# Ten small vector loads move from the sync engine's DMA queue to the scalar engine's

## The chip, the cores and the metric

The program runs on one core of one Trainium2 chip. The number that counts is the device time in microseconds of one execution. The core has five instruction streams: TensorE (PE), VectorE (DVE), ScalarE (ACT), GpSimd (POOL) and the sync engine (SP, which only issues transfers). Each stream is executed in order. An instruction that waits holds up whatever stands behind it in its own stream.

## The reference

Two layers of a streaming encoder over 1024 tokens of width 1024, with 256 memory tokens. The part that matters here is the start of layer A, and the vectors that go with it:

```
mem_n = layer_norm(mem, mem_ln_g, mem_ln_b)
u, qm, gate = split(x @ a_w_in)                      # u: 2 x 1536 channels
a, gl = split(u);  h = a * sigmoid(gl)
h = causal depthwise conv, 31 taps (a_conv_w) + a_conv_b
y_mix = silu(layer_norm(h, a_ln_g, a_ln_b))
...
y_mem = cross attention of qm into mem_n
x = layer_norm(ALPHA * x + concat(y_mix, y_mem) * silu(gate) @ a_w_out)
```

Layer B is sparse attention: an indexer scores the keys, the 256 best per query are kept, 12 heads attend to them. It ends with the same kind of output projection and LayerNorm. All of it is in float32.

## The kernel before

Every float32 matrix product is done as three products of float32r parts (hi by hi, hi by lo, lo by hi). A weight piece of 128 by 512 words is loaded (L122), rounded into `wh` by ACT (L131), and its remainder `wl` is formed by POOL (L132). There are three buffers for the raw pieces, so the fourth load of a piece has to wait until POOL has finished with the first.

The kernel starts by loading x in eight blocks of 128 tokens (`x_load`, L244, tiles `xn`). Each block is transposed on PE into a PSUM tile `px` (L249, two such tiles), then ACT writes the hi part `xhi` (L168) and DVE the lo part `xlo` (L169). The first projection needs the first four blocks, which are the first 512 tokens, and the first two weight pieces, which are the gate columns of `u_pair(0)`. Pieces three and four are the `a` columns of the same pair. `project_steps` issues the 24 products of half a projection (L149, L151, L153).

The change touches `rows_load`. It gathers the per-channel vectors as rows of two small tiles: 31 taps, conv bias, LN gain and LN bias for channels 0 to 1023 (`rows0`) and 1024 to 1535 (`rows1`), and the memory LayerNorm's gain and bias (`rows0`). They are ten loads. `rows_in` transposes them on PE (L267) and DVE copies the result into `chan` (L268). The users of `chan` are the memory tokens' LayerNorm (L290), the convolution (L423, L433) and the gate of the convolution's output (L613).

The order of the instructions on each engine isn't the order of the source. A planner runs through the program with modelled durations and gives an engine that is free the ready instruction with the highest priority, and priority follows the source. What has nothing to wait for can thus go out early on an idle engine. Before the change every transfer of the program was issued by SP. The completion of transfers is signalled over a small set of counters that are handed out in turn, and a counter that is still in use is waited for at the next issue that gets it.

Of the kernel before, what the change touches and what calls it, by code (L numbers as in the profile page):

```python
# [18 lines left out]
PSUM = bass.MemoryType.PSUM  # L19

P = 128
T = 1024
# [5 lines left out]
TAPS = 31  # L28
# [36 lines left out]
def trunk(ctx, tc, x, mem, mem_g, mem_b, a_w_in, conv_w, conv_b, ln_g, ln_b,  # L65
          a_w_mkv, a_w_out, a_pg, a_pb, b_w_in, b_w_mkv, b_w_out, b_pg, b_pb, out, dbg=None):
    nc = tc.nc
# [13 lines left out]
    # ---------------------------------------------------------------- constants  # L81
# [7 lines left out]
    # per-channel vectors, channel on the partition: taps, conv bias, LN gain, LN bias, mem gain, mem bias  # L89
# [12 lines left out]
    # PSUM banks: projections ("pj") and the rest ("pt"), from the pools of the phase  # L102
# [14 lines left out]
    # ---------------------------------------------------------------- helpers  # L117
    def split_w(src3, shape, place=None, pool_only=False):
        """Loads a [128, 512]-word piece of a weight and splits it into two float32r parts."""
        n = uid()  # L120
        raw = wp.tile(shape, F32, tag="wraw", bufs=3, name=f"wr{n}")
        nc.sync.dma_start(raw, src3)  # L122
        if place is None:
            hi = wp.tile(shape, F32R, tag="whi", bufs=6, name=f"wh{n}")
            lo = wp.tile(shape, F32R, tag="wlo", bufs=6, name=f"wl{n}")
        else:
            hi, lo = place(n)
        if pool_only:
            nc.gpsimd.tensor_copy(hi, raw)
        else:  # L130
            nc.scalar.activation(hi, raw, AF.Copy)  # L131
        nc.gpsimd.tensor_tensor(lo, raw, hi.bitcast(F32), op=OP.subtract)  # L132
        return hi, lo

    def load_cols(w, c0, n=P, pool_only=False):
        """Columns c0:c0+n of a [1024, C] weight as two pieces of four 128-row blocks."""
        res = []
        for g in range(2):
            res.append(split_w(w[g * 512:(g + 1) * 512, c0:c0 + n].rearrange("(k p) c -> p k c", p=P), [P, 4, n],
                               pool_only=pool_only))  # L140
        return res

    def project_steps(pieces, mhi, mlo, c0, n, o):
        """o[cols, n] = W^T X over the moving operand's columns c0:c0+n, one product at a time."""
        for k in range(KD):
            hi, lo = pieces[k // 4]
            wh, wl = hi[:, k % 4, :], lo[:, k % 4, :]
            xh, xl = mhi[:, k, c0:c0 + n], mlo[:, k, c0:c0 + n]
            nc.tensor.matmul(o, wh, xh, start=(k == 0), stop=False)  # L149
            yield  # L150
            nc.tensor.matmul(o, wh, xl, start=False, stop=False)  # L151
            yield
            nc.tensor.matmul(o, wl, xh, start=False, stop=(k == KD - 1))  # L153
            yield

    def run(steps):
        """All that is left of some steps, and what they return."""
        while True:
            try:
                next(steps)  # L160
            except StopIteration as end:
                return end.value
# [12 lines left out]
    def ln_moments(src):  # L175
        """Mean and 1/sqrt(var + eps) of [128, 1024] along the free axis."""
        n = uid()
        st = small.tile([P, 2, 6], F32, tag="bnst", name=f"bnst{n}")
        for i in range(2):
            nc.vector.bn_stats(st[:, i, :], src[:, i * 512:(i + 1) * 512])  # L180
        mv = small.tile([P, 2], F32, tag="bnmv", name=f"bnmv{n}")
        nc.vector.bn_aggr(mv, st)
        rs = small.tile([P, 1], F32, tag="bnrs", name=f"bnrs{n}")
        nc.scalar.activation(rs, mv[:, 1:2], AF.Sqrt, bias=eps)
        nc.vector.reciprocal(rs, rs)
        return mv[:, 0:1], rs

    def ln_stats(src):
        """Scale and bias that normalize."""
        mean, rs = ln_moments(src)  # L190
        nb = small.tile([P, 1], F32, tag="bnnb", name=f"bnnb{uid()}")
        nc.vector.tensor_scalar(nb, mean, rs, -1.0, op0=OP.mult, op1=OP.mult)
        return rs, nb
# [7 lines left out]
    def layer_norm_late(dst, src, g, b, o):  # L201
        """The same in fewer steps, written out by halves."""
# [7 lines left out]
    def transpose_in(src, hi, lo, t, f=None):  # L210
        """[128 tok, 1024] -> columns t*128.. of the transposed hi and lo operands."""
# [11 lines left out]
    # ================================================================ layer A  # L223
    SC = {}
    with ExitStack() as actx:
# [14 lines left out]
        # ---- x and the vectors  # L240
# [13 lines left out]
        def rows_load():  # L254
            nc.gpsimd.memset(rows[1][32:, :], 0.0)
            for i, sl in enumerate((slice(0, T), slice(T, CONV_CH))):
                nc.sync.dma_start(rows[i][:TAPS, :], conv_w[:, sl])
                for j, v in enumerate((conv_b, ln_g, ln_b)):
                    nc.sync.dma_start(rows[i][TAPS + j:TAPS + j + 1, :], v[sl].unsqueeze(0))
            for j, v in enumerate((mem_g, mem_b)):  # L260
                nc.sync.dma_start(rows[0][TAPS + 3 + j:TAPS + 4 + j, :], v.unsqueeze(0))
# [8 lines left out]
        # ---- memory tokens: LN, transposed  # L270
# [23 lines left out]
        def mem_k(w, h, kv=None, raw=None):  # L294
            """K^T of one head of the memory attention, into kv = [K hi | V hi | K lo | V lo] or raw = [K | V]."""
# [8 lines left out]
        def mem_v(w, h, kv=None, raw=None):  # L304
            """V of one head, likewise."""
# [13 lines left out]
        def silu_gate(pl, w, c0, dst):  # L319
            """silu of 128 gate columns, transposed, into dst [128, 1024]."""  # L320
# [6 lines left out]
        def mem_q(pl, tags, pc):  # L327
            """Queries of one head, transposed, in two parts; the products one at a time."""
# [9 lines left out]
        def mem_scores(pl, tags, q, kv, hf, banks_s):  # L338
            """Softmax over the memory tokens for half of the queries."""
# [26 lines left out]
        def mem_values(pl, tags, pn, kv, hf, sg, y, bank_pv, between=lambda ins: None):  # L366
            """Probabilities, transposed, times values, gated: half of y [128, 1024]."""
# [19 lines left out]
        # ---- gated conv input and the convolution  # L387
# [30 lines left out]
        def conv_pair(hs, i0):  # L418
            """Depthwise causal convolution of two channel tiles, taps interleaved."""
# [17 lines left out]
        def conv_stat(i):  # L437
            """Running sums over channels of the convolution less the mean of its first 128 channels."""
# [78 lines left out]
        # ---- conv LN statistics per token, then broadcast to all channels  # L517
# [22 lines left out]
        def load_y(pl, tag, src, dh, dl, gate=None, sub=None):  # L540
            """A branch in two parts, times silu(gate) where that is still to be done."""
# [23 lines left out]
        # ---- output projection of layer A  # L565
# [5 lines left out]
        def out_group(w_out, k0, yh, yl, acc, t_order, first=False, after=None, resident=None):  # L571
            """acc[tok, :] += y[:, 4 channel blocks] W_out[4 row blocks, :]."""
# [70 lines left out]
        def keep_a(hf, k):  # L643
            """Places for the last group's weights, all of which stay: four pieces where others are too."""
# [15 lines left out]
    # ================================================================ layer B  # L660
    with ExitStack() as bctx:
# [7 lines left out]
        def parts(b):  # L669
            """Key columns of a query block, cut into equal pieces of at most 512."""  # L670
# [28 lines left out]
        def gate_steps(pl, i, pool_only=False):  # L699
            """silu of 128 gate columns, transposed, into DRAM, one product at a time."""  # L700
# [10 lines left out]
        # ---- indexer  # L711
# [85 lines left out]
        def head_q(h, pc):  # L797
            """Queries of a head, scaled by scale / slope; the products one at a time."""
# [11 lines left out]
        with ExitStack() as kctx:  # L810
            bm = kctx.enter_context(pool("bm"))

            # ---- exact 256th largest score of every query, bit by bit of its order-preserving key: state is the
            # float whose key has the bits found so far, and flipping a bit of it raises it (the lower bits of a
            # negative float count down). One group of blocks is counted on the vector engine (scores >= candidate),
            # the other on the scalar engine (scaled by 2^24, signs of candidate - score): there a candidate that is
            # itself a score may be refused, so the state may end one float low, which an exact count settles.
            def threshold():
# [44 lines left out]
                # scalar engine's group: drop what is too small to be a score, try the next float  # L863
# [13 lines left out]
            # ---- distances, with a large one where a key isn't selected (ties: lowest index first)  # L877
            def select():
# [7 lines left out]
                for b in SELECT:  # L886
# [12 lines left out]
                    # as many equal ones are taken as those above leave room for  # L899
# [20 lines left out]
        # ---- sparse attention: logits over slope in PSUM, one (head, two query blocks) step after the other  # L920
        with ExitStack() as tctx:
# [15 lines left out]
            def scores(h, j):  # L937
                """Softmax of query blocks 2j and 2j + 1."""
# [28 lines left out]
            def values(h, j, pt):  # L967
                """Transposed probabilities times values, gated."""
# [22 lines left out]
                for k in range(2 * j + 1):  # L991
                    nc.tensor.matmul(po, vh[:, k, :], ph[:, k, :], start=(k == 0), stop=False)
                    nc.tensor.matmul(po, vh[:, k, :], pl[:, k, :], start=False, stop=False)  # L993
                    if k == 2 * j:
                        # the last keys: for the second block only
# [40 lines left out]
            # one head after the other, scores a step ahead of values; between the products of a head run those of the  # L1036
            # next head's queries (of the last head: a gate that is left)
# [19 lines left out]
            def filler(i):  # L1057
                """Weights and steps of what runs beside head i of the sequence."""
# [19 lines left out]
            # places in the pool: what is written first lies clear of the selection's tiles  # L1078
# [22 lines left out]
    # ---- output projection of layer B  # L1101
# [66 lines left out]
```

## Time and profile before

| | us |
|---|---|
| median of 3 runs | 1740.03 |
| lowest, highest | 1739.72, 1742.56 |
| span of the profiled execution | 1739.0 |

The span goes from the first to the last instruction. No other time is given for the profiled execution. The median lies 1.03 us above its span. PE is busy for 1677.7 us of the span, with a mean granted clock of 0.986 of full speed.

### The profile page before, as it was taken

To read this page: it belongs to the slowest core of one execution; us is meant where nothing else is said; L and a number is where in the kernel's file an instruction comes from. 1 tells how busy PE (TensorE), PEld (TensorE's weight loads), DVE (VectorE), ACT (ScalarE), POOL (GpSimd) and SP (SyncE) were. 2 spreads that over 40 slices of the span, in tenths; PEclk is the share of its full clock that TensorE was granted. 3 is DMA by queue.
4 is the path that set the end of the run, shared out by engine and by line. 5 is a ranking of instruction groups with operands and counts; after the bars stand their busy time and mean duration, and the time that the engine had idled before them with its cause. 6 is when DMAs were issued, how large, how long until landed. Compare 5 with 4: busy or idle time off the path is not lost.

```text
span 1739.0 us, 22460 instructions
## 1 busy us (share of the span) xinstructions
PE 1677.7 (96%) x8214; PEld 1385.0 (80%) x8214; DVE 1171.7 (67%) x1800; ACT 756.5 (43%) x1416; POOL 688.5 (40%) x587
## 2 busy tenths in 40 slices
PE   7999999999999998999999999879999999999997
PEld 6877888888888876887855777668898988888886
DVE  3799999999995659256154899975545655535337
ACT  3333444443433514134453678455544544542121
POOL 2344554555546337334311333343223333343233
PEclk9999999999999998999999999989999999999999
DMA  5121222212233475122320233212112121137212
GB/s 180 49 61 61 85 61 73 82 63 90 69 110 122 146 278 169 61 80 88 93 56 25 74 91 90 75 37 80 62 55 73 61 80 49 61 120 266 93 43 97
DMA packets 138941, 156.88 MB, mean 90 GB/s; under 512 B 8074, under 2 KB 108426, under 8 KB 138832
## 3 DMA queue, kind: packets, MB, share of 16 engines
q1 hardware_dynamic: 138832, 155.47, 27.6%
q8 instruction: 64, 1.05, 0.2%
q14 instruction: 45, 0.37, 0.1%
HBM read 114.81 MB, written 38.80 MB: 88 GB/s over the span
## 4 chain that ended last, share of the span: by engine, by line
PE 62%; DVE 11%; ACT 3%; issue 2%; DMA 1%; POOL 1%; SPq 0%; DVEq 0%; ACTq 0%; POOLq 0%
PE pj L149 10%; PE pj L153 10%; PE pj L151 10%; PE pj L587 5%; PE pj L586 5%; PE pj L585 5%; DVE junk L829 3%; PE pt L981 2%; PE S L778 2%; PE S L951 1%; PE S L952 1%; PE S L953 1%; PE S L777 1%; PE pv L993 1%; PE pv L997 1%
## 5 line engine op out<-in xcount | busy, mean ns | idle before, releaser
L149 PE MATMUL pj<-xhi,wh 128*128 128x512 f32 (+2 forms) x1328 | 526.2, 396 | 17.6 <-DVE ql L807 3.6
L132 POOL TENSOR_TENSOR wl<-wr,wh 128x512 fp32r<-128x512 f32 (+1 forms) x260 | 350.8, 1355 | 460.6 <-ACT wh L131 444.9
L153 PE MATMUL pj<-xhi,wl 128*128 128x512 f32 (+2 forms) x1328 | 523.7, 394 | 0.0
L151 PE MATMUL pj<-xlo,wh 128*128 128x512 f32 (+2 forms) x1328 | 522.4, 393 | 0.6 <-DVE xlo L169 0.5
L433 DVE SCALAR_TENSOR_TENSOR acc<-h,chan,acc 128x996 f32<-128x996 f32 (+27 forms) x348 | 418.5, 1263 | 16.1 <-ACT acc L423 14.8
L149 PEld LDWEIGHTS pj<-xhi,wh 128*128 128x128 f32 (+1 forms) x1328 | 250.9, 189 | 73.8 <-DVE ql L807 6.9
L153 PEld LDWEIGHTS pj<-xhi,wl 128*128 128x128 f32 (+1 forms) x1328 | 250.9, 189 | 52.4 <-issue 3.7
L151 PEld LDWEIGHTS pj<-xlo,wh 128*128 128x128 f32 (+1 forms) x1328 | 251.1, 189 | 49.7 <-issue 2.0
L131 ACT ACTIVATE wh<-wr 128x512 fp32r<-128x512 f32 x236 | 147.2, 628 | 299.3 <-PE pj L151 155.4
L585 PE MATMUL pj<-wh,xhi 128*128 128x512 f32 x384 | 150.7, 399 | 9.3 <-DVE accA L592 5.6
L586 PE MATMUL pj<-wl,xhi 128*128 128x512 f32 x384 | 150.9, 395 | 0.0
L587 PE MATMUL pj<-wh,xlo 128*128 128x512 f32 x384 | 149.2, 394 | 0.0
L961 POOL TENSOR_SCALAR t<-t,smB 128x128 f32<-128x128 f32 (+3 forms) x96 | 71.6, 747 | 177.3 <-DVE smB L960 86.1
L956 DVE CUSTOM_DVE_ANT_0 t<-S,xs 128x128 f32<-128x128 f32 (+3 forms) x96 | 70.8, 755 | 64.9 <-PE S L953 42.9
L169 DVE TENSOR_TENSOR pl<-pt,ph 128x512 fp32r<-128x512 f32 (+1 forms) x120 | 69.2, 580 | 57.6 <-ACT ph L168 56.7
L585 PEld LDWEIGHTS pj<-wh,xhi 128*128 128x128 f32 x384 | 73.5, 191 | 27.6 <-DVE accA L592 6.4
L959 ACT ACTIVATE t<-t,mxB 128x128 f32<-128x128 f32 (+3 forms) x96 | 74.1, 774 | 49.0 <-DVE mxB L958 48.9
L168 ACT ACTIVATE ph<-pt 128x512 fp32r<-128x512 f32 (+1 forms) x120 | 60.2, 508 | 73.7 <-PE pt L981 67.7
L829 DVE TENSOR_SCALAR_CACHE_REDUCE junk<-xs,cand 128x1024 bf16<-128x1024 f32 (+2 forms) x93 | 89.9, 966 | 2.2
L835 ACT ACTIVATE junka<-xs,cand 128x896 bf16<-128x896 f32 (+2 forms) x93 | 80.3, 863 | 24.2 <-DVE cand L860 22.3
L587 PEld LDWEIGHTS pj<-wh,xlo 128*128 128x128 f32 x384 | 73.3, 191 | 16.0
L586 PEld LDWEIGHTS pj<-wl,xhi 128*128 128x128 f32 x384 | 73.4, 191 | 15.5
(273 smaller groups left out, 2726.4 us busy)
## 6 DMA issues: line engine op xcount, KB each, us to landing
wr<-in_a_w_in_dram SPq DMA_DIRECT2D x88, 256.0 KB
wr<-in_b_w_in_dram SPq DMA_DIRECT2D x76, 256.0 KB
wr<-in_a_w_out_dram SPq DMA_DIRECT2D x32, 256.0 KB
wr<-in_b_w_out_dram SPq DMA_DIRECT2D x32, 256.0 KB
yraw<-yb SPq DMA_DIRECT2D x16, 512.0 KB
gb<-gB SPq DMA_DIRECT2D x15, 512.0 KB
ga<-ga SPq DMA_DIRECT2D x12, 512.0 KB
gt<-ga SPq DMA_DIRECT2D x12, 512.0 KB
```

Of the source, the lines that this page charges most:

```text
L131: nc.scalar.activation(hi, raw, AF.Copy)
L132: nc.gpsimd.tensor_tensor(lo, raw, hi.bitcast(F32), op=OP.subtract)
L149: nc.tensor.matmul(o, wh, xh, start=(k == 0), stop=False)
L151: nc.tensor.matmul(o, wh, xl, start=False, stop=False)
L153: nc.tensor.matmul(o, wl, xh, start=False, stop=(k == KD - 1))
L433: nc.vector.scalar_tensor_tensor(dst[:, s:], h[:, :T - s], w, acc[:, s:], op0=OP.mult, op1=OP.add)
L585: nc.tensor.matmul(o, yh[:, k, tsl], wh, start=(k == 0), stop=False)
L586: nc.tensor.matmul(o, yh[:, k, tsl], wl, start=False, stop=False)
L587: nc.tensor.matmul(o, yl[:, k, tsl], wh, start=False, stop=(k == 3))
L829: nc.vector.tensor_scalar(j[:, :nk(b)], xs(b), th[:, i:i + 1], None, op0=op, op1=OP.add, accum_out=c[:, i:i + 1])
L835: nc.scalar.activation(j[:, :nk(b)], xs(b), AF.Sign, bias=th[:, i:i + 1], scale=-(2.0 ** 24), accum_out=c[:, i:i + 1])
L959: nc.scalar.activation(t, t, AF.Exp, bias=mx[:, e:e + 1], scale=s, accum_out=sm[:, e:e + 1])
```

## The change

The ten loads in `rows_load` are issued by the scalar engine (`nc.scalar.dma_start`) and no longer by the sync engine. Sources, destinations, sizes and the place in the source stay. The other lines of the diff only remove comments and docstrings, which compute nothing.

```
         def rows_load():
             nc.gpsimd.memset(rows[1][32:, :], 0.0)
             for i, sl in enumerate((slice(0, T), slice(T, CONV_CH))):
-                nc.sync.dma_start(rows[i][:TAPS, :], conv_w[:, sl])
+                nc.scalar.dma_start(rows[i][:TAPS, :], conv_w[:, sl])
                 for j, v in enumerate((conv_b, ln_g, ln_b)):
-                    nc.sync.dma_start(rows[i][TAPS + j:TAPS + j + 1, :], v[sl].unsqueeze(0))
+                    nc.scalar.dma_start(rows[i][TAPS + j:TAPS + j + 1, :], v[sl].unsqueeze(0))
             for j, v in enumerate((mem_g, mem_b)):
-                nc.sync.dma_start(rows[0][TAPS + 3 + j:TAPS + 4 + j, :], v.unsqueeze(0))
+                nc.scalar.dma_start(rows[0][TAPS + 3 + j:TAPS + 4 + j, :], v.unsqueeze(0))
```

## Rows read from the trace of the kernel before

**Rows 1.** The page: busy time, share of the span and instructions of each engine.

```profile
PE 1677.7 (96%) x8214; PEld 1385.0 (80%) x8214; DVE 1171.7 (67%) x1800; ACT 756.5 (43%) x1416; POOL 688.5 (40%) x587
```

**Rows 2.** Windows: stretch, its length, busy time per engine, PE clock, DMA share, GB/s.

```profile
14.00:23.00 9.00, 8.89 (x43) 7.13 (x42) 1.81 (x2) 1.54 (x2) 1.30 (x1) 1.00 0.27 106
23.00:27.00 4.00, 0.85 (x5) 0.52 (x4) 0.00 (x0) 0.63 (x1) 0.24 (x1) 0.93 0.62 181
27.00:33.00 6.00, 6.00 (x34) 4.95 (x34) 1.23 (x1) 5.01 (x7) 3.94 (x4) 0.76 0.39 112
```

**Rows 3.** PE's waits in 0 to 60 us: total, times, longest.

```profile
PE px L249 <- DMA xn<-in_x_dram: 4.2, 1, 4.2
PE pj L149 <- ACT wh L131: 3.1, 1, 3.1
```

**Rows 4.** Issues of the sync engine in order of time: start, us, how many.

```profile
0.73 1.83 SPq L244 DMA_DIRECT2D xn<-in_x_dram  x4
2.60 1.05 SPq L122 DMA_DIRECT2D wr<-in_a_w_in_dram  x2
3.70 1.61 SPq L244 DMA_DIRECT2D xn<-in_x_dram  x2
5.35 0.71 SPq L122 DMA_DIRECT2D wr<-in_a_w_in_dram  x1
6.11 3.34 SPq L244 DMA_DIRECT2D xn<-in_x_dram  x2
9.49 0.33 SPq L257 DMA_DIRECT2D rows<-in_a_conv_w_dram  x1
...
13.81 0.23 SPq L257 DMA_DIRECT2D rows<-in_a_conv_w_dram  x1
...
21.90 0.40 SPq L122 DMA_DIRECT2D wr<-in_a_w_in_dram  x1
```

**Rows 5.** What the sync engine's issues waited for, 0 to 60 us: total, times, longest.

```profile
SPq L122 <- DMA rows<-in_a_conv_w_dram: 6.0, 2, 4.4
SPq L259 <- DMA xn<-in_x_dram: 3.0, 3, 1.0
SPq L259 <- DMA wr<-in_a_w_in_dram: 1.8, 3, 0.6
```

**Rows 6.** Windows of 2 us at the start and while the row loads run.

```profile
0.00:2.00 2.00, 0.00 (x0) 0.00 (x0) 0.00 (x0) 1.27 (x1) 1.33 (x9) 1.00 0.13 25
...
18.00:20.00 2.00, 2.00 (x11) 1.65 (x10) 0.00 (x0) 0.00 (x0) 0.00 (x0) 1.00 0.07 27
20.00:22.00 2.00, 2.00 (x12) 1.69 (x11) 0.00 (x0) 0.00 (x0) 0.00 (x0) 1.00 0.06 25
```

**Rows 7.** Sizes of the two larger row loads, from the list of transfers.

```profile
rows<-in_a_conv_w_dram SPq DMA_DIRECT2D x1, 124.0 KB
rows<-in_a_conv_w_dram SPq DMA_DIRECT2D x1, 62.0 KB
```

**Rows 8.** Timeline, several engines: start, us, instruction, idle time before it and releaser.

```profile
0.73 1.28 ACT L168 ACT_TABLE_LOAD   x1 [0.73 <-PEq L1155]
1.16 0.52 POOL L255 MEMSET rows<- 4x512 f32 x1
6.16 1.02 ACT L168 ACTIVATE xhi<-px 128x1024 fp32r<-128x1024 f32 x1 [4.15 <-PE px L249]
10.35 0.63 ACT L131 ACTIVATE wh<-wr 128x512 fp32r<-128x512 f32 x1 [1.47 <-DMA wr<-in_a_w_in_dram]
14.05 0.47 PE L149 MATMUL pj<-xhi,wh 128*128 128x512 f32 x1
26.05 0.63 ACT L131 ACTIVATE wh<-wr 128x512 fp32r<-128x512 f32 x1 [10.17 <-DMA wr<-in_a_w_in_dram]
32.27 0.94 PE L267 MATMUL pj<-ident,rows 36*128 36x36 f32 x12
```

**Rows 9.** Windows by stage after the start.

```profile
41.00:347.00 306.00, 301.27 (x1411) 250.33 (x1410) 281.12 (x261) 126.25 (x212) 151.36 (x115) 0.99 0.22 66
```

## The prediction

> **What bounds the kernel now.** I read the page first: PE is busy for 96% of the span [rows 1], so what the change is worth is decided by whether PE waits more or less. The chain of waits is followed back from the end only to about 347 us, so the start has to be read from the windows. They show PE busy for 301.27 of the 306 us from 41 to 347 us [rows 9]. From 41 us on PE hardly waits for anything, and the convolution on DVE and everything after it start from what PE has made. A shift of PE's stream at the start is therefore carried to the end, us for us. That is the first choice I make: I count only what the first 41 us gain or lose.
>
> In those 41 us PE waits 4.2 us for the first block of x, and 3.1 us, longest of all after that, for a rounded weight piece [rows 3]. This second wait is the fourth piece: ACT stands still for 10.17 us and rounds it only at 26.05 [rows 8]. Its load was issued at 21.90, after eight of the ten row loads [rows 4], because the sync engine had waited up to 4.4 us for the first conv_w load to land [rows 5]. The fourth piece is the 20th issue and the first conv_w load the 12th: 4 + 2 + 2 + 1 + 2 loads stand before it [rows 4]. The small waits fit the same count: row loads wait for x blocks and weight pieces issued eight before them [rows 5]. I read this as eight completion counters handed out in turn.
>
> Why did that conv_w load take from 9.49 to 21.9 us? Between 18 and 22 us the DMA engines are busy for 0.07 and 0.06 of the time, at 27 and 25 GB/s [rows 6]. One engine of 16 is 0.0625. So one engine alone carries the conv_w rows, 31 of them, after it has finished its share of x: 124 KB at 25 GB/s is 5.1 us, the 62 KB of the second are 2.5 us [rows 7].
>
> **The change part by part.**
>
> *Removed from SP.* Ten issues of 0.23 to 0.35 us [rows 4], about 2.6 us, and their waits. SP then reaches the fourth weight piece as soon as the first raw buffer is free. POOL forms the first remainder right behind ACT's 0.63 us at 10.35 [rows 8], so the load could go out some 9 us earlier than 21.90. At most this takes away PE's 3.1 us wait [rows 3] and the half-speed stretch behind it: PE ran 6.00 us at a mean clock of 0.76 [rows 2], which is 6.00 x 0.24 = 1.4 us. The gain is 0 to 4.5 us.
>
> A rule speaks against more than a little here. The rows say that SP stood not for its own issue time but for a landing, 4.4 us in one place [rows 5]. The Trainium skill, DMA: Bandwidth & Descriptors, section "Issuing engines are not separate DMA queues", says that transfers from all issuing engines interleave on the same DMA engines, so that a second issuer saves only the sequencer's time. By the rule the change is worth at most SP's 2.6 us, 1737.4 us, and nothing where SP has time to spare; by the rows the waits for landings count too, on whichever queue they stand.
>
> *Added to ACT.* Ten issues. The trace has none on ACT, so I take SP's 0.23 to 0.35 us for each. Where do they stand in ACT's order? ACT has nothing ready until the first transposed block at 6.16, apart from a table load [rows 8], and the row loads need no input. POOL shows what the planner does with such work: the memset of `rows`, far down in the source, runs at 1.16 [rows 8]. SP shows it too: eight row loads stand ahead of the weight piece that comes before them in the source [rows 4]. I therefore expect all ten, or nearly all, at the head of ACT's stream, ahead of `xhi` of block 0. By issue time alone they would be done at 0.73 + 10 x 0.35 = 4.2 us, before 6.16, and cost nothing.
>
> *The wait this adds.* If the counters are handed out over both queues, 20 or more issues now go through eight counters in the first 5 us, and the later ones wait for the landing of the one eight issues earlier. With SP and ACT issuing alternately, the fifth row load (the second conv_w) gets the counter of the first conv_w, and the ninth (memory gain) that of the fifth. Queued behind them on ACT are the evictions of x (L168) and the rounding of the weights (L131). For these wait DVE, POOL and PE.
>
> How late is that? Bytes start about 1.0 us after an issue: the first is at 0.73 [rows 4], and in the first 2 us the engines are busy for 0.13 x 2 = 0.26 us [rows 6]. The first conv_w load starts at about 1.9. It meets the engine's share of x. Served at once it takes 5.1 us and lands at 7.0; sharing the engine evenly with x, 10.2 us, 12.1. No row shows two queues on one engine. I take the even share, because x keeps the queue full until about 16 us, and by 18 us the share has fallen to 0.07 [rows 6]. The second conv_w is issued 0.3 us later, starts 1.0 us after that, and takes 2.5 us alone or 5.1 us shared: it lands at 15.9 to 18.5. Two more issues make 0.6 us. ACT is free between 16.5 and 19.1 if the first is shared (I take 18.3, since x and weights are still moving), and at 7.0 + 0.3 + 1.0 + 2.5 + 0.6 = 11.4 if nothing is shared.
>
> *The sum.* The first eviction moves from 6.16 to 18.3, that is +12.1. From it to the first projection it is 14.05 - 6.16 = 7.9 us [rows 8], of which 1.47 us was a wait for the first weight piece; that piece will have landed, so -1.5. PE's wait for the fourth piece is gone, since PE needs it only some 9 us after its new start: -3.1 [rows 3]. The half-speed restart of 1.4 us is saved there but paid at the new start, where PE has stood for ten us: 0. Sum +7.5 us. The profiled execution has a span of 1739.0, so 1746.5; the median of the runs is 1740.03 and I add the same: 1747.5 us, 0.43% more.
>
> *Moved transfers.* The row loads themselves are first read at 32.27 by the transposes [rows 8]. They land before that in every case, so their own lateness costs nothing; if that cover were gone, the convolution would start later.
>
> **The rivals.**
>
> *ACT isn't held up (faster).* If each queue has its own counters, or the waits end early, ACT's issues are done by 4.2 us. The fourth weight piece is early, and up to 4.5 us are won. Against it: the one engine still has to carry 186 KB of conv_w, now among x and the first two pieces. A later third block, up to 5.1 us in the even share but partly covered (x blocks wait for PSUM and evictions anyway), puts about 2 us on the start. That gives 1735.5 to 1737.5. It decides if the fifth row load doesn't wait for a transfer that lands after 6.16. For it speaks that SP's counters are the only ones the trace shows; against it, that these are so few that SP itself waits.
>
> *Hidden (same).* The planner could put the row loads behind the evictions, into ACT's idle 10.17 us before 26.05 [rows 8]. Then SP's relief (up to -4.5) stands against late conv_w bytes on the one engine, which still reach the weight pieces: between -2 and +2, 1738 to 1742. The ten issues are 2.6 us of SP's time [rows 4], so nothing is left to win where SP waits anyway. This is the case that the skill's rule above would give; no row before the change shows a second queue.
>
> *A partial block (slower, less).* If the fifth load finds another counter, ACT is held only until an x block or the first conv_w lands, at 7 to 12.1 us, and pays again later. +0.7 (11.4 - 6.16 - 4.6) to +5.
>
> The planner's order elsewhere may also move with its modelled clock. I can't price this from rows beyond a few us of either sign.
>
> **How the numbers follow.** The full block on ACT 0.45, the partial block 0.17, hidden 0.18, not held up 0.20. The likeliest's own range: ACT free between 16.5 and 19.1 gives +5.7 to +8.3; without the 1.5 us for the first piece, and with a dearer restart, +11; so 1745 to 1751. Together with the partial block and the hidden case the range reaches from 1737 to 1752, and leaves out most of the faster case and any larger reordering. Differences below 0.2%, 3.5 us, can't be told from no change here. Slower by more: 0.45 and most of the partial block, 0.58. Same: 0.22. Faster: 0.20.
>
> **What would show it.** Right: the SP rows show the fourth weight piece well before 21.90; ten DMA rows of ACT at its head, some with waits for conv_w; the first `xhi` at 16 to 19 us; the first projection at about 25 us; no wait of PE for the fourth piece; then an unchanged distance to the end. Wrong: the first `xhi` still near 6 us, or PE's total idle after 41 us changed by several us, which would mean another order.

## The result and the profile after

The changed kernel takes 1759.54 us (median of 4 runs, 1758.58 to 1762.28), the kernel before 1739.88 beside it: a ratio of 1.0119, 95% interval 1.0107 to 1.0131. That is 19.7 us more, where 7.5 were forecast and 12 were the upper end of the range. The profiled executions have spans of 1739.0 and 1760.4 us.

The page of the changed kernel, the line that answers to [rows 1]:

```profile
PE 1679.8 (95%) x8214; PEld 1387.5 (79%) x8214; DVE 1170.5 (66%) x1800; ACT 760.7 (43%) x1418; POOL 691.6 (39%) x587
```

PE is busy for 2.1 us more in a span 21.4 us longer. So nearly all of the loss is waiting.

The sync engine's issues, in the columns of [rows 4], and below them what it waited for, as in [rows 5]:

```profile
0.73 1.81 SPq L244 DMA_DIRECT2D xn<-in_x_dram  x4
8.34 0.93 SPq L122 DMA_DIRECT2D wr<-in_a_w_in_dram  x2
10.71 3.44 SPq L244 DMA_DIRECT2D xn<-in_x_dram  x2
17.74 0.38 SPq L122 DMA_DIRECT2D wr<-in_a_w_in_dram  x1
18.34 1.60 SPq L244 DMA_DIRECT2D xn<-in_x_dram  x2
21.58 9.03 SPq L122 DMA_DIRECT2D wr<-in_a_w_in_dram  x6
```

```profile
SPq L122 <- DMA rows<-in_a_conv_w_dram: 5.8, 1, 5.8
```

The row loads have left SP, but not their waits. The first weight piece, issued at 2.60 before, goes out at 8.34, because it gets the counter of a conv_w load. The fourth piece goes out at 21.58, hardly sooner than the 21.90 of before.

ACT's timeline at the start, in the columns of [rows 8]; ACTq is its issuing of transfers:

```profile
0.73 0.77 ACTq L257 DMA_DIRECT2D rows<-in_a_conv_w_dram  x2
1.52 0.32 ACTq L259 DMA_DIRECT2D rows<-in_a_conv_b_dram  x1
1.88 0.27 ACTq L259 DMA_DIRECT2D rows<-in_a_ln_g_dram  x1
5.52 0.21 ACTq L259 DMA_DIRECT2D rows<-in_a_ln_b_dram  x1
5.76 1.28 ACT L168 ACT_TABLE_LOAD   x1 [5.76 <-DMA xn<-in_x_dram]
7.61 1.02 ACT L168 ACTIVATE xhi<-px 128x1024 fp32r<-128x1024 f32 x1 [0.57 <-PE px L249]
16.79 0.21 ACTq L259 DMA_DIRECT2D rows<-in_a_conv_b_dram  x1
17.16 0.21 ACTq L259 DMA_DIRECT2D rows<-in_a_ln_g_dram  x1
17.42 1.02 ACT L168 ACTIVATE xhi<-px 128x1024 fp32r<-128x1024 f32 x1 [8.79 <-DMA rows<-in_a_conv_b_dram]
```

Five row loads stand at the head of ACT's stream, the other five from 16.79 on among the evictions. ACT evicts the first block at 7.61 and then stands for 8.79 us, held by its own sixth row load, which waits for the landing of the first tile's conv_w (the 124 KB). The 186 KB of both conv_w loads, issued at 0.73, have landed by 16.79: 186 KB in some 15 us are 12.7 GB/s, half of the 25 GB/s of [rows 6].

PE's waits in 0 to 60 us, against [rows 3]:

```profile
PE px L249 <- DVE xlo L169: 7.8, 2, 7.0
PE px L249 <- DMA xn<-in_x_dram: 6.9, 3, 5.6
...
```

The 3.1 us for the fourth piece are gone. In their place PE waits for the evictions and for x. The first projection starts at 23.1 (14.05 in [rows 8]).

PE's waits in 60 to 770 us, and below them the window that answers to [rows 9]:

```profile
PE pj L149 <- ACT ga L325: 10.6, 4, 4.9
PE pt L289 <- ACT mf L290: 7.0, 2, 4.8
```

The first of these lines in the kernel before; no wait for `mf` stands in its list:

```profile
PE pj L149 <- ACT ga L325: 2.6, 3, 1.5
```

The window:

```profile
41.00:347.00 306.00, 293.85 (x1355) 243.22 (x1355) 279.50 (x263) 121.76 (x203) 145.12 (x111) 0.97 0.20 62
```

PE is busy for 293.85 of these 306 us, 7.4 less than before. The prediction had taken this stretch as one that only hands the start on.

**Where the time was lost.** In a table that I worked out from the traces, each matmul is counted from the end of the program, among those of its line and shape, and set against the same one in the kernel before. Its start from the span's beginning in the one, less that in the other, gives how far PE is behind, in us. Each entry is the median over 20 us of the kernel before that begin at the time in the head. The lower kernels belong to the experiments.

```
                                    60    160    440    520    760    900   1200   1500
changed kernel                     6.7   12.1   11.4   18.4   20.4   20.4   20.7   20.7
e1  order after, loads before      1.1    6.5    5.7   12.7   13.6   13.6   14.4   14.4
e2  order before, loads after      3.0    3.0    3.0    3.0    2.1    2.1    2.6    2.5
e9  loads after, rows split       -1.7    3.9    4.9    7.4    5.4    5.4    6.6    6.5
e7  loads before, rows split      -6.5   -6.7   -6.7   -6.7   -7.1   -7.1   -6.9   -6.9
e13 before, recounted             -3.3   -4.3   -4.3   -4.2   -5.0   -5.1   -5.3   -5.4
e10 order after, 50-138 us        -1.2    3.1    3.1    3.2    2.5    2.5   -3.0   -3.2
e11 order after, 138-644 us       -3.3    2.3    1.6    6.5    4.9    4.9   -2.0   -2.2
e12 order after, 644-1115 us      -2.6   -2.7   -2.7   -4.1   -5.5   -5.5  -11.3  -11.5
e14 order after, 50-1115 us       -3.7    2.0    1.3    8.3    7.3    7.3    1.4    1.2
e15 changed, recounted             5.2   11.9   11.2   17.3   16.4   16.4   17.4   17.4
e17 changed, order before from 50  5.5    5.7    5.7    4.7    5.1    5.1    1.0    0.7
```

The changed kernel loses 6.7 us by 60 us. It loses 5.4 more between 60 and 160, 7.0 between 440 and 520 and 2.0 up to 760, and gives 0.7 back in between. From there to 1500 us the distance stays within 0.3. One profile stands behind each row, and executions differ: e13 has the order and the transfers of before, yet its profiled execution is 3.3 us ahead at 60 us, while its median is that of before. Steps within a row are therefore surer than the first column.

### The profile page after: what moved, and what is told of

Its sections match the earlier page's. It is cut to its first block, busy times and chain, and to the rows that moved or that the text cites. A ratio compares the mean times of both kernels' runs of the same rounds, so it can differ in the third digit from the quotient of the medians.

```text
span 1760.4 us, 22470 instructions
## 1 busy us (share of the span) xinstructions
PE 1679.8 (95%) x8214; PEld 1387.5 (79%) x8214; DVE 1170.5 (66%) x1800; ACT 760.7 (43%) x1418; POOL 691.6 (39%) x587
## 4 chain that ended last, share of the span: by engine, by line
PE 53%; DVE 11%; issue 3%; ACT 3%; POOL 1%; DMA 1%; DVEq 0%; ACTq 0%; POOLq 0%
PE pj L149 8%; PE pj L151 7%; PE pj L153 7%; PE pj L586 5%; PE pj L585 5%; PE pj L587 5%; DVE junk L829 3%; PE pt L981 2%; PE S L778 2%; PE S L951 1%; PE S L952 1%; PE S L777 1%; PE S L953 1%; PE pv L997 1%; PE pv L993 1%
## 5 line engine op out<-in xcount | busy, mean ns | idle before, releaser
L433 DVE SCALAR_TENSOR_TENSOR acc<-h,chan,acc 128x1021 f32<-128x1021 f32 (+28 forms) x348 | 417.9, 1265 | 20.2 <-ACT acc L423 19.0
L829 DVE TENSOR_SCALAR_CACHE_REDUCE junk<-xs,cand 128x1024 bf16<-128x1024 f32 (+2 forms) x93 | 89.9, 967 | 2.2
```

The source lines that it names most:

```text
L433: nc.vector.scalar_tensor_tensor(dst[:, s:], h[:, :T - s], w, acc[:, s:], op0=OP.mult, op1=OP.add)
L829: nc.vector.tensor_scalar(j[:, :nk(b)], xs(b), th[:, i:i + 1], None, op0=op, op1=OP.add, accum_out=c[:, i:i + 1])
```

## The experiments

Two theories stood against each other. Theory A: the queue costs what it does to the start, and the rest comes from the planner's new order of the whole program. Rival B: the order is of no weight, and the late start grows on its way. In e1 to e6 the planned program is kept on every engine, and at most its first 22 transfers are changed. The diffs that list transfers show their order and not the program's text. In them x0 to x7 are blocks of x, w1 to w4 weight pieces, cw, cb, g and b the rows of conv_w, conv_b and LN gain and bias (0 or 1: which tile), mg and mb the memory LN's.

**e1_order_after_loads_before.** The changed kernel's program with the transfers of before, all on SP.

```
- cw1 x0 x1 cw0 x2 cb0 x3 g0 w1 b0 w2 cb1 x4 g1 x5 b1 w3 mg x6 mb x7 w4    rows on ACT
+ x0 x1 x2 x3 w1 w2 x4 x5 w3 x6 x7 cw0 cb0 g0 b0 cw1 cb1 g1 b1 w4 mg mb    all on SP
```

> All compute instructions in the order of the changed kernel; the first 22 transfers on the sync engine in the order of the kernel before. Theory A (the held-up scalar engine costs the start some 6.5 us, and the other 13 to 14 us come from the planner's other order later on): the first convolution step stands near 53 us as before, the end is 12 to 15 us late: 1752 to 1755 us. Rival B (the order costs nothing, a late start grows on its way to the end): 1740 to 1742 us.

Measured: 1755.4 us, ratio 1.0088 (1.0073 to 1.0103), +15.4. The first projection is at 13.9 us as before, and the table shows the same steps as in the changed kernel, +5.4 by 160 and +7.0 by 520. The order alone costs this.

**e2_order_before_loads_after.** The reverse: the program of before with the two lists exchanged.

> All compute instructions in the order of the kernel before; the first 22 transfers as in the changed kernel, ten of them on the scalar engine, at the same places in its stream. Theory A: the second block's eviction stands near 17 us, the first convolution step 6 to 7 us late, and this is carried unchanged: 1745 to 1748 us. Rival B: 1757 to 1761 us.

Measured: 1744.56 us, 1.003 (1.002 to 1.004), +4.6. ACT stands for 8.93 us in the same place, the first projection is at 22.9, and the distance at 60 us is carried on unchanged (3.0 there, 2.5 at 1500). +15.4 and +4.6 make 20.0; the change costs 19.7. B falls.

**e3_wait_only.** The kernel before, in which the eviction of the second block also waits for the eighth block of x.

```
  xhi of block 1:   wait(PE px)
+                   wait(x7 landed)
```

> The kernel before, in its own order and with its own transfers, but the eviction of the second x block also waits until the eighth x block has landed (about 16.5 us). Theory A: a late start alone, 3 to 7 us, carried unchanged: 1743 to 1747 us. Rival B: 1750 us or more.

Measured: 1744.54 us, 1.0028 (1.0017 to 1.0038), +4.5. ACT stands for 9.63 us, with every row load still on SP. A stand of ACT of this length at this place costs what the queue costs.

**e4_piece4_first.** The kernel before, with the fourth weight piece issued ahead of the row loads.

```
- ... x7 cw0 cb0 g0 b0 cw1 cb1 g1 b1 w4 mg mb
+ ... x7 w4 cw0 cb0 g0 b0 cw1 cb1 g1 b1 mg mb
```

> The kernel before, with the fourth weight piece issued ahead of the ten row loads on the sync engine. If PE's wait of 3.1 us for this piece is worth its length and is carried to the end, with the half-speed stretch behind it: 1735.5 to 1737 us. If the start is covered by something later: 1739 to 1741 us.

Measured: 1743.64 us, 1.002 (1.0011 to 1.0029), +3.6: a miss of the wrong sign. ACT's and SP's timelines:

```profile
16.91 0.63 ACT L131 ACTIVATE wh<-wr 128x512 fp32r<-128x512 f32 x1 [2.14 <-DMA wr<-in_a_w_in_dram]
28.49 0.63 ACT L131 ACTIVATE wh<-wr 128x512 fp32r<-128x512 f32 x1 [10.95 <-DMA wr<-in_a_w_in_dram]
```

```profile
11.25 0.38 SPq L122 DMA_DIRECT2D wr<-in_a_w_in_dram  x1
16.90 0.30 SPq L257 DMA_DIRECT2D rows<-in_a_conv_w_dram  x1
...
24.79 6.07 SPq L122 DMA_DIRECT2D wr<-in_a_w_in_dram  x4
```

```profile
SPq L257 <- DMA wr<-in_a_w_in_dram: 5.3, 1, 5.3
```

The fourth piece is rounded at 16.91, 9 us sooner than in [rows 8]. But the fifth is now the one that stands behind conv_w. ACT waits 10.95 us for it with an eviction (L407) queued behind, and PE waits 4.6 us for that eviction. The edit also did more than its list shows. The transfers keep their counters, and the fourth piece has the same one as the first conv_w load. So SP waits 5.3 us for the piece to land, and the row loads go out from 16.90 on, in place of 9.49. How much of the 3.6 us comes from that delay, and how much from the fifth piece's place behind conv_w, e4 doesn't separate. It shows that one piece put ahead isn't enough.

**e5_split_order_before** and **e7_split_planned.** All loads on SP; each conv_w load is issued as 16 and 15 rows. In e5 all else keeps the order of before, in e7 the planner orders anew.

```
-                nc.sync.dma_start(rows[i][:TAPS, :], conv_w[:, sl])
+                for a, z in ((0, 16), (16, TAPS)):
+                    nc.sync.dma_start(rows[i][a:z, :], conv_w[a:z, sl])
```

> The kernel before with its own order on every engine and its own queue; only the two conv_w row loads are each issued as two loads, of 16 and of 15 rows, so that more engines than one carry them. 24 transfers then go through the eight counters at the start. If conv_w's bytes on the one engine are what makes SP stand and what delays the next weight piece (theory), the landing of conv_w moves up by 3 us or more, the fourth piece lands earlier, PE's wait for it (3.1 us) goes, and the time is 1735.5 to 1737. If SP's stand has another cause (the mere number of issues through the counters), two more issues make it 1740 to 1742.

> The same split of conv_w into 16 and 15 rows on the sync engine, written in the source, so that the planner orders everything anew. Theory (the order costs by itself, and small edits at the start draw a new one): the start gains what the split with the held order gains, a few us, and the rest of the program moves by some amount of its own, up to 15 us either way, seen as waits for ACT behind 100 us. Rival (an order costs only where the start is late): the time equals that of the split with the held order within 2 us.

Measured: e5 1735.8 us, 0.9984 (0.9975 to 0.9994); e7 1735.48, 0.9982 (0.997 to 0.9993). Both beat the kernel before, by 3 us. SP's issues in e5:

```profile
9.24 1.25 SPq L257 DMA_DIRECT2D rows<-in_a_conv_w_dram  x2
...
18.31 0.40 SPq L122 DMA_DIRECT2D wr<-in_a_w_in_dram  x1
```

The fourth piece goes out at 18.31 in place of 21.90, though two more issues stand before it. SP's waits for conv_w [rows 5] and PE's wait for the piece [rows 3] are gone from the lists. The packet records of the traces show the transfers themselves. (They give start, length and size of every packet that the DMA engines moved; a row load has one packet for each row, a weight piece one for each 512 bytes.) The 31 packets of 2 KB of the second conv_w load run one after another from 21.86 to 24.51 us in the kernel before; in e5 they lie between 15.41 and 17.38, up to ten at a time. The one engine is the cause. In e7 PE stays, at the times of the table, within 0.6 us of its lead of 6.5, so the new order that theory A expected to cost something of its own cost nothing here.

**e6_loads_after_not_held.** As e2, but the five later row loads stand on ACT behind the eviction of the fourth block.

```
- ACT: cw1 cw0 cb0 g0 b0 | xhi 0 | cb1 g1 | xhi 1 | b1 | wh | mg | xhi 2 | wh | mb | xhi 3
+ ACT: cw1 cw0 cb0 g0 b0 | xhi 0 | xhi 1 | wh | xhi 2 | wh | xhi 3 | cb1 g1 b1 mg mb
```

> The order of the kernel before on every engine; the ten row loads on the scalar engine as in the changed kernel, but the five later ones stand behind the eviction of the fourth x block, so that ACT isn't held by them between the first and the second eviction. If ACT's stand (8.8 us) is what the queue itself costs at the start, the first projection comes at 16 to 17 us in place of 22.9 and the time is 1738 to 1741. If the late first projection comes from x and weights sharing the one engine with conv_w, or from the first weight pieces that wait for conv_w's counter, the first projection stays at 20 us or later and the time at 1743 to 1745.

Measured: 1745.55 us, 1.004 (1.0025 to 1.0055), +6.5. ACT's timeline:

```profile
7.39 1.03 ACT L168 ACTIVATE xhi<-px 128x1024 fp32r<-128x1024 f32 x1 [0.57 <-PE px L249]
10.08 1.02 ACT L168 ACTIVATE xhi<-px 128x1024 fp32r<-128x1024 f32 x1 [1.67 <-PE px L249]
18.02 0.63 ACT L131 ACTIVATE wh<-wr 128x512 fp32r<-128x512 f32 x1 [6.92 <-DMA wr<-in_a_w_in_dram]
```

ACT evicts the second block at 10.08 and then waits for the first weight piece. SP could issue that one at 8.24 only, when the first of the two conv_w loads had landed (5.7 us in SP's list of waits). It is rounded almost ten microseconds later, at 18.02. The packet records show what it waits for: of the 1024 packets of the first two pieces, 960 start by 11.6 us, and the other 64, a sixteenth, start one at a time between the packets of the larger conv_w load or behind them; the last ends at 18.09. ACT's stand and SP's stand are two doors behind the same bytes, and opening one gains nothing.

**e8_gpsimd_planned** and **e9_scalar_split_planned.** The ten loads on GpSimd's queue, and on ACT's with the rows split; the planner free in both.

```
-                nc.scalar.dma_start(...)
+                nc.gpsimd.dma_start(...)                                                # e8, all ten
+                for a, z in ((0, 16), (16, TAPS)): nc.scalar.dma_start(rows[i][a:z, :], conv_w[a:z, sl])   # e9, conv_w
```

> The ten row loads on the GpSimd engine's queue in place of the scalar engine's, the planner free. Theory: GpSimd's own work at the start is small, so the loads hold neither SP nor ACT, and what the start costs is the share of the one engine, 0 to 4 us; the new order adds its own part, so that the time can lie anywhere from 1738 to 1757, with the waits behind 100 us telling the part. Rival (ACT's stand at the start is the only cost of the change, order costs nothing): 1738 to 1741.

> The changed kernel, ten vectors on the scalar engine's queue, with conv_w's two row loads issued as 16 and 15 rows each; the planner free. If the 31 rows on one engine are what makes the scalar queue dear at the start (theory), ACT's 8.8 us stand and the 5.8 us that SP waits for the first weight piece shrink to 2 us or less and the first projection comes at 14 to 17 us in place of 23.1. The time is then 1735 to 1741 if the order drawn is as good as that of before, and up to 1755 if it is as poor as the changed kernel's. If two queues by themselves are dear, the first projection stays behind 20 us.

Measured: e8 1742.67 us, 1.0023 (1.0014 to 1.0033): by the same comparison PE is 4.8 us ahead of before at 60 us and 2.2 behind at 780. e9 1748.34 us, 1.0063 (1.0043 to 1.0083). ACT and SP at e9's start:

```profile
8.25 0.38 ACTq L258 DMA_DIRECT2D rows<-in_a_conv_w_dram  x1
8.67 1.02 ACT L168 ACTIVATE xhi<-px 128x1024 fp32r<-128x1024 f32 x1 [1.26 <-PE px L249]
```

```profile
SPq L122 <- DMA rows<-in_a_conv_w_dram: 0.9, 1, 0.9
```

The second block is evicted at 8.67 in place of 17.42, and the first projection is at 14.2. At 60 us e9 is 1.7 us ahead of before, so with the rows split the start loses nothing against the kernel before. Against e7, which has the split rows on SP, it is 4.8 us behind there (one profile each): ACT's queue may still cost something. All of e9's loss against the kernel before comes later: 5.6 by 160 and 2.5 between 440 and 520, in the same two places.

**e10_order_first, e11_order_middle, e12_order_late** put one stretch of the order after into the kernel before; **e14_order_after_50us** puts all three; **e13_before_recounted** is their control. The cuts are where both planned programs have issued the same set of instructions, and the semaphores had to be counted anew across them. (A semaphore is a counter by which one instruction waits for others; the number to wait for depends on the order in which they add to it.)

```
  program(order before), semaphores counted anew
+ instructions of one stretch in the order after     e10 50-138 us, e11 138-644, e12 644-1115, e14 all three, e13 none
```

> The kernel before with its transfers and its start as they are; only one stretch of the program, from about 50 us to the first transposes of the memory tokens near 138 us, is in the order that was planned for the changed kernel. The rest keeps the order of before. If the order's cost lies in single places (theory), this stretch gives what PE's waits differ by there: 7.5 us in place of 3.9 by 138 us, so +2 to +5: 1742 to 1745. If the cost needs the whole order (rival: it comes from the sum of many small shifts, or from the start), 1739 to 1741.

> As the one before, with the next stretch alone in the changed kernel's order: from the memory tokens near 138 us to the end of layer A's first branch near 644 us. By the waits of PE for ACT's ga and mf (15.4 us in place of 1.0 there, of which part is won back) this stretch carries most of the order's cost: +7 to +12, 1747 to 1752. Rival as before: 1739 to 1741.

> As before, with the stretch from about 644 us to the first attention values near 1115 us alone in the changed kernel's order. From the first instruction at 644 us to that at 773 us the kernel with the changed order took 4.7 us longer than the one before. If the order there costs that by itself, 1743 to 1745; if it was only the lateness of the middle stretch that came to light there, 1739 to 1741. The three stretches' costs should add up to the 15.4 us of the whole order if each has its own places.

> The kernel before, every instruction in its order and on its queue, with its semaphores counted anew as in the three stretch kernels: an instruction that nothing waits for signals nothing, the others add 1. The control for those three. If the new counting is what made the late parts shorter (theory), this one takes about 6 us off the kernel before: 1731.5 to 1734.5, with 341 us from the start of line 216 to that of line 951 (344 in before). Then the three stretches cost about +4, +10 and 0 over it. If it comes out at 1738 to 1741, the stretches' own times stand, and the order's cost isn't in any of the three.

> All three stretches together: from about 50 us on the order of the changed kernel, the first 50 us and the transfers those of before, counted anew. If the stretches add up, the control's time plus the sum of the three differences (about +13): 1744 to 1749. If the order's cost needs the first 50 us as well, the control's time plus 0 to 5: 1732 to 1738.

| | us | ratio to before | interval |
|---|---|---|---|
| e10 | 1736.34 | 0.9987 | 0.9977 to 0.9998 |
| e11 | 1742.42 | 1.0015 | 1.0004 to 1.0026 |
| e12 | 1731.72 | 0.9957 | 0.9942 to 0.9972 |
| e13 | 1740.63 | 1.0007 | 0.9997 to 1.0017 |
| e14 | 1744.45 | 1.0029 | 1.002 to 1.0039 |

Read by their end times these were misses: the three differ from before by -2.7, +3.4 and -7.3 us, which don't add up to 15. The counting anew isn't the reason, since e13 equals the kernel before. The table shows what is. Up to 760 us the places cost what they cost in e1: e10 loses 4.3 between 60 and 160, e11 5.6 there and 4.9 between 440 and 520, e14 5.7 and 7.0. (The first place lies across the cut at 138 us: either stretch by itself brings most of its cost, and both together no more.) PE's waits in 60 to 770 us in e11, with all else in the order of before:

```profile
PE pj L149 <- ACT ga L325: 7.2, 3, 3.6
PE pt L289 <- ACT mf L290: 7.0, 2, 4.8
```

These are the waits of the changed kernel again. Between 900 and 1200 us all four kernels then win 5.5 to 6.9 us, on a stretch that has the order of before in e10 and e11. More on it in the last section.

**e15_after_recounted** and **e17_after_order_before_from_50us.** The changed kernel counted anew, and the same with the order of before from 50 us on.

```
  program(order after), its own transfers and first 50 us, semaphores counted anew      e15
+ instructions from 50 us to 1115 us in the order before                                e17
```

> The changed kernel as it is, counted anew. If the counting is worth the same in every order, 1759.5 less what the control takes off the kernel before: 1752 to 1755. If the counting acts only where the order of before stands, 1757 to 1761.

> The changed kernel up to about 50 us, with its transfers on the scalar engine's queue and its order; from there to the first attention values near 1115 us every engine has the order of the kernel before. Semaphores counted anew, so the control is the changed kernel so counted, 1758.4. If the order behind 50 us costs by its two places near 130 and 490 us (theory: 4.7 and 7.0 us in the profiles, 2 more near 600), PE's instructions stand some 7 us behind those of the kernel before at 60 us and still 6 to 8 us at 900 us, and the time is 1742 to 1748, less by up to 6 if the counting stretch runs short as in the four kernels with other stretches. If the lateness of the start is what grows on its way (rival), PE is 18 us or more behind at 900 us and the time 1753 to 1760.

Measured: e15 1758.43 us, 1.0115 (1.0098 to 1.0132); e17 1742.14, 1.0012 (1.0002 to 1.0021). e15 is 19.3 us above the kernel before that ran beside it, e17 2.0 above its own. Of the 17.3 us between them, 5.1 lie between 900 and 1200 us, where e17 gains 4.1 and e15 loses 1.0; the other 12.2 are the later order's (11.3 by the table at 900 us). The start's lateness stays, 5.5 us at 60 and 5.1 at 900. PE's waits in e17 from 60 to 770 us show the places gone:

```profile
PE pt L289 <- ACT co L432: 2.5, 1, 2.5
...
PE pj L149 <- ACT ga L325: 1.8, 2, 1.5
```

**e16_split_recounted.** The split of e7, counted anew.

```
  e7's source
+ semaphores counted anew, no instruction moved
```

> The split rows as planned on the sync engine (1735.5 by itself) with the semaphores counted anew. If the two gains add, 1727 to 1731; if the counting gives nothing, 1734 to 1737.

Measured: 1733.89 us, 0.9972 (0.996 to 0.9984), beside 0.9982 for e7: the intervals overlap, and no gain of the counting shows.

## Why the prediction was wrong

**The failed step: "I count only what the first 41 us gain or lose", and that the order elsewhere can't be priced "beyond a few us of either sign".** The sign was right and the start was nearly right, but the order behind 50 us costs the larger part, 14.0 of the 20.7 us by which PE is behind at 1500 us. The sum had put this term at nothing. It is shown from both sides: e1 has this cost without the queue, e17 has the queue without this cost.

How an order costs is seen at the second place. ACT's timeline in the changed kernel, and what PE waits for:

```profile
498.59 1.28 ACT L359 ACT_TABLE_LOAD   x1 [3.10 <-DVE mx L356]
...
501.44 1.28 ACT L325 ACT_TABLE_LOAD   x1
502.74 0.60 ACT L325 ACTIVATE ga<-pj 128x512 f32<-128x512 f32 x1
...
503.38 0.58 PE L149 MATMUL pj<-mhi,wh 128*128 128x256 f32 x1 [4.89 <-ACT ga L325]
```

The same place in e17, with the order of before:

```profile
492.35 0.58 ACT L325 ACTIVATE ga<-pj 128x512 f32<-128x512 f32 x1
492.94 1.28 ACT L359 ACT_TABLE_LOAD   x1
```

The eviction of a gate (`ga`) was planned ahead of the softmax's exponentials in the one and behind them in the other. Behind them it waits for the maximum from DVE (3.10 us), two table loads of 1.28 and the exponentials, and PE waits 4.89 us for the bank that it would empty. At the first place, ACT's timeline of the changed kernel, and PE's wait:

```profile
139.91 1.04 ACT L448 ACTIVATE sumd<-co 128x1024 f32<-128x1024 f32 x1
140.86 1.04 ACT L449 ACTIVATE sumsq<-co 128x1024 f32<-128x1024 f32 x1
141.81 1.19 ACT L423 ACTIVATE acc<-h,chan 128x1024 f32<-128x1024 f32 x1
142.94 0.54 ACT L290 ACTIVATE mf<-pt,chan 128x256 f32<-128x256 f32 x1
...
143.54 0.69 PE L289 MATMUL pt<-ident,mt 128*128 128x128 f32 x2 [4.79 <-ACT mf L290]
```

The same place in e17:

```profile
139.43 0.57 ACT L290 ACTIVATE mf<-pt,chan 128x256 f32<-128x256 f32 x1
139.88 1.06 ACT L448 ACTIVATE sumd<-co 128x1024 f32<-128x1024 f32 x1
```

Two sums and a convolution's start, 3.0 us together, stand ahead of the memory tokens' `mf`, for which PE waits 4.8 us. In the order of before `mf` stands ahead of all three. That the planner put them so because its modelled clock had moved is what I suppose; no run shows its reasons.

**Carried to the end, us for us.** Right, for a start. At the table's times behind 60 us e2 changes by no more than 0.9 and e7 by 0.6; e3, by the same comparison, is 4.7 us behind at 60 and 5.1 at 1500.

**All ten at the head of ACT's stream; the first eviction at 18.3.** Half right. Five stood there and the first eviction went at 7.61; the second, behind the sixth row load, went at 17.42. Since the first projection needs four blocks, it comes to nearly the same: 23.1 us where 25 was forecast. That it does is luck: the placing behind the 18.3 is not the one that the planner chose.

**The wait this adds, and the even share of the one engine.** Right: 16.79 us for the landing of both conv_w loads lies inside the forecast 15.9 to 18.5. The smaller load went first, which the forecast had the other way round; the sum of both is the same.

**Removed from SP: 0 to 4.5 us.** PE's wait of 3.1 us did go, but SP gained nothing: a row load on either queue takes its turn among the same eight counters, and SP then waited 5.8 us for conv_w with its first weight piece. I had put this wait on ACT alone. The Trainium skill's rule that was weighed there would have given 1737.4 us or no change. Its first half agrees with the trace, since both queues' bytes meet on the one engine (12.7 GB/s for conv_w where 25 was seen alone). What the rule does not speak of is the issuing engine's wait, and that decided the start.

**The sum, +7.5.** The profiled execution is 6.7 behind at 60 us, and e15's 5.2. By medians the queue with the order of before costs 4.6, with ends by the interval at 3.5 and 7.0. The term was some 1 to 3 us too large and of the right kind. What had been missing was a term for the order.

## What to carry to other kernels

Where a planner orders a program, an edit that touches only its first microseconds can reorder all of it. Price that as a term of its own, from nothing to 15 us in this kernel, and tell it from the edit by an experiment that holds the order fixed. A transfer put on a computing engine's queue brings its wait for a completion counter with it, and everything behind it on that engine is held (8.8 us here). Where a small load is slow, look at how many DMA engines carry it before moving it: splitting 31 rows into 16 and 15 gave the 3 us that no queue gave.

## What the runs showed of the hardware

**One engine for 31 rows.** The share of 0.06 to 0.07 at 25 to 27 GB/s of [rows 6] is these row loads alone. In the packet records of the kernel before, the 31 packets of 4 KB of the first conv_w load follow one another from 16.77 to 21.70 us, 0.16 us each. In e9, where the rows come as 16 and 15, the first 16 packets of 2 KB are through in 0.33 us (2.45 to 2.78), up to nine at a time. The Trainium skill, DMA: Bandwidth & Descriptors, section "Why a DMA increments its semaphore by 16 and not by 1", says that the number of engines is the largest up to 16 that divides the slowest dimension, which is 1 for 31 rows; these records agree.

**Two queues on one engine took turns packet by packet.** In the changed kernel conv_w's packets on ACT's queue run one at a time, those of 2 KB from 1.66 to 7.79 us and those of 4 KB from 8.10 to 15.82. From 14.2 us to 15.8 each is followed by one packet of 512 bytes of the sync engine's weight pieces, a pair in 0.18 us. Of the 1024 packets of the first two pieces, 960 start by 11.6 us. Of the 64 that are left, more than 40 start only when the row loads are through, at 16.76, and then follow 0.02 us apart; the last ends at 17.81. So these two pieces land after conv_w, though all but a sixteenth of them has long arrived.

**A small DVE instruction can take eight times its time.** In layer B, DVE counts scores in 31 rounds, with integer steps of 128x6 between them, while POOL forms the remainders of weight pieces. DVE's and POOL's timelines in e13:

```profile
1039.62 1.00 DVE L858 TENSOR_TENSOR no<-c,lim 128x6 int32<-128x6 f32 x1
...
1042.06 1.29 DVE L857 TENSOR_SCALAR nxt<-cand 128x6 int32<-128x6 int32 x1
...
1044.96 0.17 DVE L858 TENSOR_TENSOR no<-c,lim 128x6 int32<-128x6 f32 x1
```

```profile
1039.32 1.29 POOL L132 TENSOR_TENSOR wl<-wr,wh 128x512 fp32r<-128x512 f32 x1
...
1042.03 1.29 POOL L132 TENSOR_TENSOR wl<-wr,wh 128x512 fp32r<-128x512 f32 x1
```

Such a step takes 0.17 us by itself, and these two take 1.00 and 1.29 where they meet POOL's 1.29 us. Both end with POOL's instruction (1040.62 and 1040.61; 1043.35 and 1043.32). The Trainium skill, SBUF — State Buffer, section "SBUF: two separate sides", says that DVE and GpSimd share a port pair as an exclusive lock, which a DVE instruction takes when it is in a two-port mode or reads two SBUF inputs. These rows look like it: L858 reads two tiles. L857 reads one, and no run here shows its mode; neither was tested by itself.

What stays open: the counting's first to last instruction (L829) takes 123.2 us in e13 and in the kernel before, 123.3 in the changed kernel, and 117.3 to 119.5 in e10, e11, e12, e14 and e17, though in e10 and e11 the order of that stretch is that of before. In e12 these steps meet POOL less often (L857 334 ns on average, 407 in e13). Why the mixed kernels all fall in that better phase was not found. It is most of why e12 is the fastest kernel of all, and I would not count on it.
